# Moving the first pair's weight preparation from the gate product into the output projection

## The chip, the cores and the metric

The kernel runs on one core of one Trainium2 chip. The metric is device time in microseconds (us) of one execution; lower is better. Before the change three timed runs gave a median of 456.75 us (456.43 to 457.58).

The engines are named as in the profile: PE (matrix multiply), PEld (its weight loads), DVE (vector engine), ACT (scalar engine), POOL (GpSimd) and SP (which here only issues DMAs).

## The reference, cut to what matters

One layer of a hybrid decoder: a combined input projection, a block-sparse attention branch and a gated linear recurrence branch, a sigmoid merge, an output projection added to the residual, and at the end a gated per-layer embedding. The change touches only the last two lines:

```python
        merged = jax.nn.sigmoid(gate_a) * ya + jax.nn.sigmoid(gate_b) * yb
        h = h + merged.astype(dt) @ w_out[i]                      # output projection, 512 x 1024 by 1024 x 1024

        ple = (p[i] @ w_ple[i]) * jax.nn.sigmoid(h @ w_ple_gate[i])   # embedding (K = 256) and the gate's product
        h = h + ple
```

## The kernel before, in words

Everything is kept transposed: 1024 features in eight blocks of 128 partitions, 512 tokens along the free axis. Each fp32 matrix product is made from three fp32r matmuls: both operands are split into a high and a low part (ACT copies x to the rounded type for the high part, DVE subtracts it from x for the low part), and hi*hi, lo*hi and hi*lo are added up in PSUM. In names, `h` and `l` at the end stand for the two parts: `w40h`, `w40l` are the parts of the fourth weight set of pair 0.

**Output projection** (the loop `for i, n in enumerate(PAIRED)`): eight blocks in the order h0, h4, h1, h5, h2, h6, h3, h7, each 24 matmuls of 512 columns. After each block DVE adds the residual (`hf`), and `pairs_of_h` makes sums and splits of the two blocks of a pair (tiles `b`, `bl`, `bt`, `bu`) that the gate's product will use.

**The gate's product** (the loop `for p in range(4)`) uses a seven-product scheme: output blocks p and p+4 form a pair, the inner dimension and the tokens are halved, and seven products of 12 matmuls of 256 columns replace eight. The products are numbered 1 to 7. They add up in three PSUM banks, `ba` (1, 2), `bb` (6, 7, 4) and `bc` (5, 3). Between certain products a partial sum must be read out of a bank before the next product adds to it: after product 1 ACT copies `ba` (`keep`), after product 6 DVE makes `keep` from `bb`, after product 7 DVE makes `keep2` (L1214), and an output that is complete is read by DVE (L1159) before the next product of that bank. PE follows the hand-written `order`; for pair 0 it is E0, 1, 5, 6, 2, 7, E1, 4, 3, where E0 and E1 are the small embedding products of six matmuls of 512 columns. `merge` finishes an output: sum, sigmoid on ACT, times the embedding (L1163), plus `hf` (L1164, on POOL, for the last pair on DVE), DMA out.

**The weights of a pair** (`pairs_of_weights`): two raw 512 KB blocks (`wf72` to `wf79` for the four pairs) are loaded by DMAs that POOL's queue issues into four buffers. From them come seven sets: `w1` (products 1 and 2, straight from the first block), the sums `s12` (products 5 and 6; first on POOL, L1046, then on DVE, L1047) and `s34` (products 7 and 3; first on POOL, L1053, then on DVE, L1054), and `w4` (product 4, straight from the second block). Each set is split by ACT (L1037) and DVE (L1038). For pair 0 the sets `w3` and `w4` carry a dependency, order only, that keeps them behind the last step of `pairs_of_h`.

PE's order is fixed by the program text. The order on the other engines comes from a scheduler that ranks by program order, priorities (`AHEAD`) and such order-only dependencies. Each engine runs its queue strictly in order, so an instruction that waits holds up everything behind it.

Of the kernel before, what the change touches and what calls it, by code (L numbers as in the profile page):

```python
# [15 lines left out]
OP = mybir.AluOpType  # L16
# [49 lines left out]
def hybrid_layer_kernel(  # L66
# [961 lines left out]
    def pairs_of_weights(p):  # L1028
        r0, r1 = wraw[late[1] + 2 * p], wraw[late[1] + 2 * p + 1]
        a11, a12, a21, a22 = [r[:, 4 * i:4 * i + 4] for r in (r0, r1) for i in range(2)]  # L1030
        s12 = pb[:, 6:8].rearrange("p a (k c) -> p a k c", k=4)
        s34 = pb[:, 8:10].rearrange("p a (k c) -> p a k c", k=4)

        def both(src, tag, name, shape, late_=False):
            h_ = unit(tag[0], name + "h", R, shape)
            l_ = unit(tag[1], name + "l", R, shape)
            first = A.activation(h_, src, AF.Copy)  # L1037
            second = V.tensor_tensor(l_, src, h_.bitcast(F32), op=OP.subtract)  # L1038
            if late_:
                held(first)  # L1040
                behind(first, edge[-2])
                behind(second, edge[-1])
            return h_, l_

        w1 = both(r0, ("wh", "wl"), f"w1{p}", (128, KD, 128))
        G.tensor_tensor(s12[:, 0], a21, a22, op=OP.add)  # L1046
        second = V.tensor_tensor(s12[:, 1], s12[:, 0], a11, op=OP.subtract)  # L1047
        if p:
            behind(second, edge[-1])
        wt[p] = {1: [t[:, 0:4] for t in w1], 2: [t[:, 4:8] for t in w1]}  # L1050
        yield
        w2 = both(s12, ("wh", "wl"), f"w2{p}", (128, 2, 4, 128))
        G.tensor_tensor(s34[:, 0], a11, a21, op=OP.subtract)  # L1053
        V.tensor_tensor(s34[:, 1], a12, s12[:, 1], op=OP.subtract)  # L1054
        wt[p].update({5: [t[:, 0] for t in w2], 6: [t[:, 1] for t in w2]})
        yield
        w3 = both(s34, ("wh", "wl"), f"w3{p}", (128, 2, 4, 128), p == 0)
        wt[p].update({7: [t[:, 0] for t in w3], 3: [t[:, 1] for t in w3]})
        yield
        w4 = both(a22, ("YB", "YB"), f"w4{p}", (128, 4, 128), p == 0)  # L1060
        wt[p][4] = w4
        yield

    firsts = {}
# [62 lines left out]
    for i, n in enumerate(PAIRED):  # L1127
        ws = weight(w_o[n])
        xres = unit("T", f"xres{n}")
        nc.sync.dma_start(xres, xT[n])  # L1130
        ps = bank("mm", f"h{n}")
        mm3(ps, ws[0], ws[1], mh, ml, KD)
        hf[n] = unit("H", f"hf{n}")
        with tc.high_priority(offset=AHEAD if n == 7 else 0):
            V.tensor_tensor(hf[n], ps, xres, op=OP.add)
        if i == 6:
            small_weights(0)
        if n < 4:
            halves = pairs_of_h(n)
        next(halves)  # L1140
        if i == 3:
            for k in range(2):
                nc.sync.dma_start(pb[:, 8 + k], pT[:, k])
                h_ = unit("A", f"ph{k}", R)
                l_ = unit("A", f"pl{k}", R)
                split(h_, l_, pb[:, 8 + k])
                ph.append(h_)
                pl.append(l_)
        if i == 5:
            preps[0] = pairs_of_weights(0)  # L1150
        if i >= 5:
            w_load(late[1] + i - 3)
        if 5 <= i < 7:
            next(preps[0])

    def merge(n, c, ps, pes, t, plus=None):
        if plus is not None:
            with tc.high_priority(offset=AHEAD):
                V.tensor_tensor(t[:, c], ps, plus, op=OP.add)  # L1159
            ps = t[:, c]  # L1160
        A.activation(t[:, c], ps, AF.Sigmoid)  # L1161
        yield
        V.tensor_tensor(t[:, c], t[:, c], pes[:, c], op=OP.mult)  # L1163
        (V if n % 4 == 3 else G).tensor_tensor(t[:, c], t[:, c], hf[n][:, c], op=OP.add)  # L1164
        nc.sync.dma_start(out[n][:, c], t[:, c])

    for p in range(4):
# [29 lines left out]
        for step in order:  # L1197
# [4 lines left out]
            elif step == "E0r":  # L1202
                ple(pe0, n0, rh)
            elif step == "E0l":
                ple(pe0, n0, lh)
            else:
                product(step)
            with tc.high_priority(offset=AHEAD):
# [4 lines left out]
                elif step == 7:  # L1213
                    V.tensor_tensor(keep2, bb, keep[:, lh], op=OP.add)  # L1214
            if step == 2:
                ends[2] = merge(n0, lh, ba, pe0, t0)
                next(ends[2])
            elif step == 4:
                ends[4] = merge(n1, lh, bb, pe1, t1, keep[:, lh])
                next(ends[4])  # L1220
            elif step == 3:
                ends[3] = merge(n0, rh, bc, pe0, t0, keep[:, rh])
                next(ends[3])
            if 5 in order[:order.index(step) + 1] and 7 in order[:order.index(step) + 1] and "c22" not in ends:
                ends["c22"] = merge(n1, rh, bc, pe1, t1, keep2)
                next(ends["c22"])
            ready = {2: ("E0", "E0l"), 3: ("E0", "E0r"), 4: ("E1",), "c22": ("E1",)}
            for e in list(ends):
                if ends[e] is not None and any(x in order[:order.index(step) + 1] for x in ready[e]):
                    next(ends[e], None)  # L1230
                    ends[e] = None
            if p == 0 and step == 1:
                next(preps[0])
            if p == 0 and step == 6:
                next(preps[0])
                small_weights(n1, True)
            if p == 1 and step in (5, 7):
                small_weights(n0 + 1 if step == 5 else n1 + 1, True)
            if p < 3 and step == 2:
# [73 lines left out]
```

## Time and profile before

| what | before |
|---|---|
| median of 3 runs | 456.75 us (456.43 to 457.58) |
| profiled execution | 456.08 us, span of its instructions 454.2 us, 1.9 us around it |
| PE busy | 446.4 us (98%) |
| DVE / ACT / POOL busy | 335.0 / 289.0 / 59.0 us |
| granted TensorE clock | 1.00 |
| output projection, blocks h2, h6, h3, h7 | 373.5 to 395.3 us |
| pair 0 of the gate's product | 395.3 to 410.6 us |
| last matmul starts | 449.80 us |

Times inside the trace count from the start of the span. In a timeline each row is start, duration, engine, line, operation, output<-inputs, shape; what stands in brackets is the engine's idle time before it and who ended it. Rows of one engine that follow each other closely overlap a little, so the cost of an instruction in a full queue is the distance to the next start and not its duration. Buffer numbers are left out of names: `hf` is any of the eight `hf` tiles.

### The profile page before, as it was taken

How to read it: one execution, taken by the hardware profiler on the slowest of the kernel's cores; microseconds unless marked ns; L12 is line 12 of the kernel's file. 1: busy time of each engine (PE TensorE's matmuls, PEld its weight loads, DVE VectorE, ACT ScalarE, POOL GpSimd, SP SyncE). 2: the span in 40 equal slices, each digit the busy share in tenths (PEclk: the TensorE clock that was granted, in tenths of full speed). 3: DMA queues.
4: the chain of work that ended last, by engine and by line, in shares of the span. 5: the costliest groups of instructions: out<-in, count | busy, mean ns of one | idle time of the engine just before them, and what ended most of it. 6: DMA issues, size and time to landing. Idle time of an engine off the chain costs nothing. (4 is left out here: it accounts for less than half of the span.)

```text
span 454.2 us, 8517 instructions
## 1 busy us (share of the span) xinstructions
PE 446.4 (98%) x3186; PEld 374.4 (82%) x3186; DVE 335.0 (74%) x679; ACT 289.0 (64%) x560; POOL 59.0 (13%) x97
## 2 busy tenths in 40 slices
PE   9999999999999999999999999999999999989996
PEld 8888888788888888878887888878888888879995
DVE  5869593876898795949976875454479769888844
ACT  5958564737679985969877996783234434365421
POOL 1000100000000000010000000101220113133520
PEclk9999999999999999999999999999999999999999
DMA  7802333257492536152435353554731542222111
GB/s 247 330 1 95 139 110 111 93 194 180 184 248 66 179 78 210 35 164 95 142 103 157 123 141 117 163 148 139 267 95 53 180 139 92 94 100 86 48 48 47
DMA packets 32713, 59.53 MB, mean 131 GB/s; under 512 B 7072, under 2 KB 18592, under 8 KB 32672
## 3 DMA queue, kind: packets, MB, share of 16 engines
q0 software_dynamic: 9056, 32.51, 21.3%
q1 hardware_dynamic: 23472, 26.47, 19.8%
q8 instruction: 25, 0.41, 0.4%
q14 instruction: 16, 0.13, 0.1%
q10 hardware_dynamic: 144, 0.01, 0.0%
HBM read 48.74 MB, written 4.98 MB: 118 GB/s over the span
## 5 line engine op out<-in xcount | busy, mean ns | idle before, releaser
L224 ACT ACTIVATE wh<-wf 128x1024 fp32r<-128x1024 f32 (+1 forms) x70 | 67.0, 957 | 63.2 <-issue 9.8
L225 DVE TENSOR_TENSOR wl<-wf,wh 128x1024 fp32r<-128x1024 f32 (+1 forms) x70 | 77.9, 1112 | 34.0 <-ACT wh L224 33.7
L264 POOL DMA_DIRECT2D wf<-in_w_tr_dram x30 | 15.9, 529 | 171.9 <-DVE wl L225 105.8
L290 PE MATMUL ga<-xh,wh 128*128 128x512 f32 x64 | 25.4, 396 | 0.1
L828 ACT ACTIVATE pb<-pb,ps 128x128 f32<-128x128 f32 (+3 forms) x32 | 17.7, 553 | 11.8 <-DVE ps L826 11.6
L290 PE MATMUL gb<-xh,wh 128*128 128x512 f32 x64 | 25.1, 393 | 0.0
L290 PE MATMUL ga<-xh,wl 128*128 128x512 f32 x64 | 24.9, 390 | 0.0
L290 PE MATMUL ga<-xl,wh 128*128 128x512 f32 x64 | 24.9, 389 | 0.0
L290 PE MATMUL gb<-xl,wh 128*128 128x512 f32 x64 | 24.9, 389 | 0.0
L290 PE MATMUL gb<-xh,wl 128*128 128x512 f32 x64 | 24.9, 389 | 0.0
L290 PE MATMUL h<-mh,wh 128*128 128x512 f32 x64 | 24.9, 389 | 0.0
L290 PE MATMUL h<-ml,wh 128*128 128x512 f32 x64 | 24.9, 389 | 0.0
L290 PE MATMUL h<-mh,wl 128*128 128x512 f32 x64 | 24.9, 389 | 0.0
L826 DVE CUSTOM_DVE_ANT_0 pb<-s,bias 128x128 f32<-128x128 f32 (+3 forms) x28 | 13.0, 495 | 10.5 <-PE lpa L559 5.4
L1161 ACT ACTIVATE sg<-sg 128x256 f32<-128x256 f32 x12 | 4.9, 414 | 20.3 <-DVE sg L1159 20.3
L830 ACT ACTIVATE pb<-pb,ps 128x128 f32<-128x128 f32 (+3 forms) x32 | 16.3, 550 | 0.2 <-DVE ps L829 0.2
L538 ACT ACTIVATE hx<-hx 128x512 f32<-128x512 f32 x24 | 14.8, 623 | 1.4 <-DVE hx L537 1.3
L264 POOL DMA_DIRECT2D wf<-in_w_up_dram x16 | 8.6, 539 | 53.7 <-DVE wl L225 50.8
L833 DVE STREAM_TRANSPOSE pb<-pb 128x512 f32<-128x512 f32 x20 | 13.8, 696 | 2.0 <-ACT pb L830 2.0
L264 POOL DMA_DIRECT2D wf<-in_w_tok_dram x8 | 4.4, 550 | 79.5 <-DVE wl L225 67.6
L290 PEld LDWEIGHTS ga<-xh,wh 128*128 128x128 f32 x64 | 12.0, 188 | 3.3 <-DVE bg3s L487 0.5
L290 PEld LDWEIGHTS gb<-xh,wh 128*128 128x128 f32 x64 | 12.0, 188 | 2.8 <-DVE hk L513 0.4
(941 smaller groups left out, 1427.6 us busy)
## 6 DMA issues: line engine op xcount, KB each, us to landing
wf<-in_w_tr_dram POOLq DMA_DIRECT2D x30, 512.0 KB, 4.5
wf<-in_w_tok_dram POOLq DMA_DIRECT2D x8, 512.0 KB, 3.5
wf<-in_w_up_dram POOLq DMA_DIRECT2D x16, 256.0 KB, 3.0
wf<-in_w_o_dram POOLq DMA_DIRECT2D x8, 512.0 KB, 4.3
wf<-in_w_g_dram POOLq DMA_DIRECT2D x8, 512.0 KB, 3.6
wf<-in_w_tok_dram SPq DMA_DIRECT2D x6, 512.0 KB, 6.9
pb<-pb SPq DMA_DIRECT2D x64, 48.0 KB, 2.9
bias<-in_ed_dram SPq DMA_DIRECT2D x8, 256.0 KB, 4.6
```

The source lines that it names most:

```text
L224: A.activation(hi, src, AF.Copy)
L225: V.tensor_tensor(lo, src, hi.bitcast(F32), op=OP.subtract)
L264: (G if len(wraw) >= FAR else nc.sync).dma_start(raw, ap)
L290: dense.append(PE.matmul(ps, a[:, k, :], b[k], start=(n == 0), stop=(n == tot - 1)))
L538: A.activation(x, x, AF.Exp)
L826: in_order(V.tensor_tensor_reduce(p_, s_[:, so:so + nk], T[j][:, nk - 1::-1], -1.0, 3e38, OP.add, OP.min, st[:, 0:1]))
L828: A.activation(p_, p_, AF.Exp, bias=st[:, 0:1], scale=-1.0, accum_out=st[:, 1:2])
L830: A.activation(p_, p_, AF.Copy, scale=st[:, 2:3])
L833: V.transpose(z[:, :, b_, :].rearrange("p b (n c) -> p b n c", c=32), pb[:, b_].rearrange("p (n b c) -> p b n c", b=4, c=32))
L1161: A.activation(t[:, c], ps, AF.Sigmoid)
```

## The change

In `pairs_of_weights`, pair 0 now takes its own way after the sets 1, 5 and 6: it makes set 4 at once (in buffers of tag `Q`), then set 7 alone (tag `SG`), then set 3 alone, called `w5` here (tags `wh`, `wl`), and only set 3 carries the order-only dependency. The generator's steps are called ahead of the matmuls of blocks i = 5, 6 and 7 (h6, h3, h7) instead of behind the blocks 5 and 6 and inside pair 0. The embedding weights of n = 4 (`pwh4`, `pwl4`) are made at i = 7 instead of after product 6. One more thing is changed: in the last pair the left half of the embedding product (E0l) writes to a bank of its own (`pe3l`, tag `mm`) instead of the bank that holds the right half. No matmul is added or taken away.

```diff
@@ pairs_of_weights
-        w3 = both(s34, ("wh", "wl"), f"w3{p}", (128, 2, 4, 128), p == 0)
+        if p == 0:
+            wt[p][4] = both(a22, ("Q", "Q"), f"w4{p}", (128, 4, 128))
+            yield
+            wt[p][7] = both(s34[:, 0], ("SG", "SG"), f"w3{p}", (128, 4, 128))
+            yield
+            wt[p][3] = both(s34[:, 1], ("wh", "wl"), f"w5{p}", (128, 4, 128), True)
+            yield
+            return
+        w3 = both(s34, ("wh", "wl"), f"w3{p}", (128, 2, 4, 128))
         wt[p].update({7: [t[:, 0] for t in w3], 3: [t[:, 1] for t in w3]})
         yield
-        w4 = both(a22, ("YB", "YB"), f"w4{p}", (128, 4, 128), p == 0)
-        wt[p][4] = w4
+        wt[p][4] = both(a22, ("YB", "YB"), f"w4{p}", (128, 4, 128))
         yield
@@ for i, n in enumerate(PAIRED)
         nc.sync.dma_start(xres, xT[n])
+        if i == 5:
+            preps[0] = pairs_of_weights(0)
+            next(preps[0])
+        elif i == 6:
+            next(preps[0])
+            next(preps[0])
+            small_weights(0)
+        elif i == 7:
+            next(preps[0])
+            small_weights(4)
         ps = bank("mm", f"h{n}")
         mm3(ps, ws[0], ws[1], mh, ml, KD)
...
-        if i == 6:
-            small_weights(0)
...
-        if i == 5:
-            preps[0] = pairs_of_weights(0)
         if i >= 5:
             w_load(late[1] + i - 3)
-        if 5 <= i < 7:
-            next(preps[0])
@@ merge: pes is now a function that gives the bank
-        V.tensor_tensor(t[:, c], t[:, c], pes[:, c], op=OP.mult)
+        V.tensor_tensor(t[:, c], t[:, c], pes()[:, c], op=OP.mult)
@@ for p in range(4)
             elif step == "E0l":
-                ple(pe0, n0, lh)
+                pe2 = bank("mm", f"pe{n0}l")
+                ple(pe2, n0, lh)
...
-            if p == 0 and step == 1:
-                next(preps[0])
             if p == 0 and step == 6:
                 next(preps[0])
-                small_weights(n1, True)
```

**Place one: DVE between block h3's residual add and that of h7.** `hf3` and `hf7` are the residual adds; `w4x` are the weights of product 4 of pair x; `pb` rows of L1085 (L1092 after) are token differences of `hf3`. Before:

```order
L1135 TENSOR_TENSOR hf3_4261<-h3_4236,xres3_4234 128x512
L1085 TENSOR_TENSOR pb_70<-hf3_4261 128x256
L1038 TENSOR_TENSOR w20l_4278<-pb_70,w20h_4277 128x1024
L225 TENSOR_TENSOR b2l_4172<-hf3_4261,b2h_4171 128x256
L225 TENSOR_TENSOR bt3l_4271<-pb_70,bt3h_4270 128x256
L1135 TENSOR_TENSOR hf7_4312<-h7_4287,xres7_4285 128x512
```

Now:

```order
L1152 TENSOR_TENSOR hf3_4276<-h3_4251,xres3_4234 128x512
L1092 TENSOR_TENSOR pb_70<-hf3_4276 128x256
L1125 TENSOR_TENSOR pwl4_4297<-pb_70,pwh4_4296 128x512
L1038 TENSOR_TENSOR w20l_4237<-pb_70,w20h_4236 128x1024
L1038 TENSOR_TENSOR w41l_4483<-wf75_4232,w41h_4482 128x512
L225 TENSOR_TENSOR b2l_4172<-hf3_4276,b2h_4171 128x256
L225 TENSOR_TENSOR bt3l_4281<-pb_70,bt3h_4280 128x256
L1038 TENSOR_TENSOR w42l_4641<-wf77_4486,w42h_4640 128x512
L1152 TENSOR_TENSOR hf7_4325<-h7_4300,xres7_4289 128x512
```

Three subtractions of 512 columns stand here that stood behind product 6 before: the embedding's `pwl4`, and the product-4 weights of pairs 1 and 2. The last needs the raw block `wf77`. Two more (`w40l` and, of half its width, `w30l`) stand one block earlier, ahead of the residual add of h2.

**Place two: DVE from the copy after product 6 of pair 0 to the first completed output.** `keep0` is that copy; L1214 (L1226 now) makes `keep2`; L1159 (L1170 now) reads a completed output out of PSUM. Before:

```order
L1212 TENSOR_TENSOR keep0_4330<-g01_4324,keep0_4330 128x256
L1038 TENSOR_TENSOR w40l_4380<-wf73_4136,w40h_4379 128x512
L1118 TENSOR_TENSOR pwl4_4385<-pb_70,pwh4_4384 128x512
L1047 TENSOR_TENSOR pb_70<-pb_70,wf74_4182 128x512
L1038 TENSOR_TENSOR w11l_4405<-wf74_4182,w11h_4404 128x1024
L1038 TENSOR_TENSOR w41l_4479<-wf75_4232,w41h_4478 128x512
L1163 TENSOR_TENSOR sg0_4328<-sg0_4328,pe0_4326 128x256
L1054 TENSOR_TENSOR pb_70<-wf74_4182,pb_70 128x512
L1214 TENSOR_TENSOR pb_70<-g01_4324,keep0_4330 128x256
L1038 TENSOR_TENSOR w21l_4435<-pb_70,w21h_4434 128x1024
L1038 TENSOR_TENSOR w42l_4637<-wf77_4482,w42h_4636 128x512
L1159 TENSOR_TENSOR sg4_4329<-g02_4325,pb_70 128x256
```

Now:

```order
L1224 TENSOR_TENSOR keep0_4343<-g01_4337,keep0_4343 128x256
L1038 TENSOR_TENSOR w50l_4389<-pb_70,w50h_4388 128x512
L1047 TENSOR_TENSOR pb_70<-pb_70,wf74_4182 128x512
L1038 TENSOR_TENSOR w11l_4409<-wf74_4182,w11h_4408 128x1024
L1054 TENSOR_TENSOR pb_70<-wf74_4182,pb_70 128x512
L1174 TENSOR_TENSOR sg0_4341<-sg0_4341,pe0_4339 128x256
L1226 TENSOR_TENSOR pb_70<-g01_4337,keep0_4343 128x256
L1038 TENSOR_TENSOR w21l_4439<-pb_70,w21h_4438 128x1024
L1170 TENSOR_TENSOR sg4_4342<-g02_4338,pb_70 128x256
```

Between `keep0` and `keep2` seven instructions stood and now five do; between `keep2` and the first completed output two stood and now one does.

**Place three: POOL's queue at the raw blocks of pairs 1 to 3.** L1046 and L1053 are POOL's sums for the weight sets, L264 the loads. Before:

```order
L264 DMA wf75_4232<-in_w_g_dram 128x1024
L264 DMA wf76_4283<-in_w_g_dram 128x1024
L1046 TENSOR_TENSOR pb_70<-wf75_4232 128x512
L1053 TENSOR_TENSOR pb_70<-wf74_4182,wf75_4232 128x512
L264 DMA wf77_4482<-in_w_g_dram 128x1024
L264 DMA wf78_4640<-in_w_g_dram 128x1024
L1164 TENSOR_TENSOR sg0_4328<-sg0_4328,hf0_3981 128x256
L264 DMA wf79_4642<-in_w_g_dram 128x1024
```

Now:

```order
L264 DMA wf75_4232<-in_w_g_dram 128x1024
L1053 TENSOR_TENSOR pb_70<-wf74_4182,wf75_4232 128x512
L264 DMA wf76_4287<-in_w_g_dram 128x1024
L264 DMA wf77_4486<-in_w_g_dram 128x1024
L1046 TENSOR_TENSOR pb_70<-wf75_4232 128x512
L264 DMA wf78_4644<-in_w_g_dram 128x1024
L264 DMA wf79_4646<-in_w_g_dram 128x1024
L1175 TENSOR_TENSOR sg0_4341<-sg0_4341,hf0_3981 128x256
```

L1053 of pair 1 moves up, ahead of the loads of `wf76` and `wf77`, and the load of `wf79` now stands ahead of the first `sg0` sum. The buffers rotate in another order too: `wf77` goes where `wf72` lay (last read by `w10l`), `wf78` where `wf75` lay (last read by `w41l` and POOL's L1046 of pair 1), `wf79` where `wf74` lay (last read by DVE's L1054 of pair 1). On ACT the split `w43h`, which waits for `wf79`, changes places with `w31h` and stands ahead of it; behind both come one sigmoid and the copy `keep1`.

More of the change, by code (lines that the diff above doesn't have):

```diff
@@ L1215, in hybrid_layer_kernel @@
             if step == 2:
-                ends[2] = merge(n0, lh, ba, pe0, t0)
+                pe2 = pe0
+                ends[2] = merge(n0, lh, ba, lambda: pe2, t0)
                 next(ends[2])
             elif step == 4:
-                ends[4] = merge(n1, lh, bb, pe1, t1, keep[:, lh])
+                ends[4] = merge(n1, lh, bb, lambda: pe1, t1, keep[:, lh])
                 next(ends[4])
             elif step == 3:
-                ends[3] = merge(n0, rh, bc, pe0, t0, keep[:, rh])
+                ends[3] = merge(n0, rh, bc, lambda: pe0, t0, keep[:, rh])
                 next(ends[3])
             if 5 in order[:order.index(step) + 1] and 7 in order[:order.index(step) + 1] and "c22" not in ends:
-                ends["c22"] = merge(n1, rh, bc, pe1, t1, keep2)
+                ends["c22"] = merge(n1, rh, bc, lambda: pe1, t1, keep2)
                 next(ends["c22"])
```

## The prediction

> **What bounds the kernel now.** I read the page first (span, busy shares, clock), then PE's own waits in the last 125 us, then PE's timeline at each of them, then the queues of the engines named there.
>
> ```profile
> span 454.2 us, 8517 instructions
> PE 446.4 (98%) x3186; PEld 374.4 (82%) x3186; DVE 335.0 (74%) x679; ACT 289.0 (64%) x560; POOL 59.0 (13%) x97
> PEclk9999999999999999999999999999999999999999
> ```
>
> PE is the bound, at full granted clock, and the change keeps all its matmuls. So it can only win the gaps between matmuls, and only from the region it touches. PE's waits after 330 us:
>
> ```profile
> PE g L1184 <- DVE pb L1214: 1.1, 1, 1.1
> PE g L1184 <- DVE sg L1159: 0.9, 1, 0.9
> PE g L1184 <- ACT keep L1210: 0.2, 1, 0.2
> ```
>
> Three waits, all in the gate's product. These rows count from the modelled end of the last matmul; the time really lost shows in the distance of the starts, in PE's timeline:
>
> ```profile
> 396.63 0.28 PE L1184 MATMUL g<-b0h,w10h 128*128 128x256 f32 x1
> ...
> 404.75 0.39 PE L290 MATMUL pe<-pl,pwh 128*128 128x512 f32 x1
> 404.98 0.39 PE L290 MATMUL pe<-ph,pwl 128*128 128x512 f32 x1
> 406.50 0.39 PE L1184 MATMUL g<-bu0h,w40h 128*128 128x256 f32 x1 [1.12 <-DVE pb L1214]
> ...
> 407.92 0.28 PE L1184 MATMUL g<-bt3h,w40l 128*128 128x256 f32 x1
> 409.11 0.39 PE L1184 MATMUL g<-bl0h,w30h 128*128 128x256 f32 x1 [0.92 <-DVE sg L1159]
> 409.33 0.28 PE L1184 MATMUL g<-bl0l,w30h 128*128 128x256 f32 x1
> ...
> 413.41 0.28 PE L1184 MATMUL g<-bt3h,w21l 128*128 128x256 f32 x1
> 413.87 0.39 PE L1184 MATMUL g<-bl0h,w11h 128*128 128x256 f32 x1 [0.18 <-ACT keep L1210]
> ...
> 448.79 0.28 PE L1184 MATMUL g<-bl3h,w13l 128*128 128x256 f32 x1
> 449.11 0.38 PE L290 MATMUL pe<-ph,pwh 128*128 128x256 f32 x1
> ```
>
> A 512-column matmul follows the last after 0.23 (404.75 to 404.98), a 256-column one after 0.12 (34 steps from 409.33 to 413.41), and the first after a stall holds PE 0.10 longer (409.11 to 409.33). The losses:
> - Before product 4 of pair 0: 406.50 - 404.98 - 0.23 + 0.10 = 1.39.
> - Before product 3 of pair 0: 409.11 - 407.92 - 0.12 + 0.10 = 1.17.
> - Before product 2 of pair 1: 413.87 - 413.41 - 0.12 + 0.10 = 0.44.
> - Before E0l of pair 3: 449.11 - 448.79 - 0.12 + 0.10 = 0.30.
>
> Together 3.30 us. That is the ceiling of the gain; what follows is how much of it stays.
>
> **Products 4 and 3 of pair 0: DVE's queue.** Both waits end with a DVE instruction that stood behind weight splits:
>
> ```profile
> 401.21 0.42 DVE L1212 TENSOR_TENSOR keep<-g,keep 128x256 f32<-128x256 f32 x1 [1.05 <-PE g L1184]
> ...
> 402.75 0.68 DVE L1047 TENSOR_TENSOR pb<-pb,wf 128x512 f32<-128x512 f32 x1
> 403.36 1.22 DVE L1038 TENSOR_TENSOR w11l<-wf,w11h 128x1024 fp32r<-128x1024 f32 x1
> 404.49 0.68 DVE L1038 TENSOR_TENSOR w41l<-wf,w41h 128x512 fp32r<-128x512 f32 x1
> ...
> 406.03 0.41 DVE L1214 TENSOR_TENSOR pb<-g,keep 128x256 f32<-128x256 f32 x1
> 406.36 1.76 DVE L1038 TENSOR_TENSOR w21l<-pb,w21h 128x1024 fp32r<-128x1024 f32 x1
> ...
> 408.64 0.41 DVE L1159 TENSOR_TENSOR sg<-g,pb 128x256 f32<-128x256 f32 x1
> ```
>
> In a full queue a 512-column subtraction costs 0.61 (402.75 to 403.36), a 1024-column one 1.13 (403.36 to 404.49), a 256-column one 0.34 (406.03 to 406.36, rounded up). `keep` at 401.21 was started by PE, so the clock starts there. With the new queue (place two) `keep2` starts at 401.21 + 0.34 + 3 x 0.61 + 1.13 + 0.34 = 404.85 instead of 406.03, and ends at 405.26. PE took it 0.06 after its end before (406.44 to 406.50), so 405.32; PE is ready at 404.98 + 0.23 = 405.21. Left over: 0.11 and perhaps the slow first matmul, **0.15** of 1.39.
>
> Then `w21l`, then the first completed output: 404.85 + 0.34 + 1.13 = 406.32, its end and hand-over 406.79. PE comes to product 3 at 405.32 + 0.10 + 12 x 0.12 = 406.86, so nothing is left if `w21l` takes 1.22. It took 1.76 before, because POOL was at work: at that length 407.33, and 0.5 is left. Which? Rows where DVE and POOL meet:
>
> ```profile
> 374.45 1.57 POOL L1046 TENSOR_TENSOR pb<-wf 128x512 f32<-128x512 f32 x1 [3.07 <-DMA wf<-in_w_g_dram]
> 374.78 1.52 DVE L1097 TENSOR_TENSOR pb<-hf,hf 128x256 f32<-128x256 f32 x1
> 376.22 2.31 DVE L225 TENSOR_TENSOR wl<-wf,wh 128x1024 fp32r<-128x1024 f32 x1
> 378.82 0.57 POOL L264 DMA_DIRECT2D wf<-in_w_g_dram  x1 [1.38 <-DVE wl L225]
> ...
> 427.40 0.88 DVE L1047 TENSOR_TENSOR pb<-pb,wf 128x512 f32<-128x512 f32 x1
> 427.69 1.19 POOL L1164 TENSOR_TENSOR sg<-sg,hf 128x256 f32<-128x256 f32 x1
> ...
> 433.19 0.74 POOL L1164 TENSOR_TENSOR sg<-sg,hf 128x256 f32<-128x256 f32 x1 [4.31 <-DVE sg L1163]
> ```
>
> With POOL first, a DVE instruction of 0.42 took 1.52 (1.1 lost). With DVE first, POOL's sum took 1.19 instead of 0.74. DVE reads PSUM at 401.21 in its usual 0.42. After the change POOL's `sg0` sum stands behind the load of `wf79`, which waits for L1054's end (403.90 + 0.68 = 404.6). A load starts 0.29 after the end of what it waits for (378.53 to 378.82) and holds POOL for 0.57, so the sum is due near 405.4 and `w21l` at 405.2: DVE first. I take the short one and leave **0.1** of 1.17.
>
> The Trainium skill, "SBUF — State Buffer", section "Who interferes with whom", says that a VectorE instruction with two SBUF inputs and a GpSimd instruction that reads SBUF exclude each other, whoever issues first holding the pair to its end. The rows above agree in both orders. By that rule the remainder at product 3 would be nothing; by a mere repeat of the 1.76 row it would be 0.5 and the gain 0.4 smaller. The rule also speaks against the change, since POOL's L1053 of pair 1 now meets a full DVE queue.
>
> **Blocks h6, h3, h7: what the earlier place costs.** The work moved must fit into DVE's idle time:
>
> ```profile
> 390.03 0.69 DVE L1135 TENSOR_TENSOR hf<-h,xres 128x512 f32<-128x512 f32 x1 [0.48 <-PE h L290]
> ...
> 395.47 0.69 DVE L1135 TENSOR_TENSOR hf<-h,xres 128x512 f32<-128x512 f32 x1 [1.39 <-PE h L290]
> ...
> 397.81 0.42 DVE L225 TENSOR_TENSOR bt3l<-pb,bt3h 128x256 fp32r<-128x256 f32 x1
> ```
>
> Added ahead of `hf7`: five subtractions of 512 columns, 5 x 0.61 = 3.05, and one meeting with POOL (L1053), 1.1. Idle there: 0.48 + 1.39 = 1.87. So `hf7` slips from 395.47 by 2.3 and the token split `bt3l` ends at 398.23 + 2.3 = 400.5. PE wants it in the eleventh matmul of product 6, at 396.63 + 34 x 0.12 = 400.71. It just fits; each 0.1 more than 0.15 goes to PE. If the meeting with POOL falls into a gap or a PSUM read, 1.1 is to spare; if a second one is added, 0.9 is lost. I take **0.1**. ACT's added splits lie in its long waits and are costed at nothing: ACT was 64% busy. The moved splits themselves are hidden under the 24 matmuls of each block; if that cover were gone they would cost the 3.05.
>
> **Product 2 of pair 1: ACT behind a load.** `keep1` frees the bank:
>
> ```profile
> 410.79 1.06 ACT L1037 ACTIVATE w31h<-pb 128x1024 fp32r<-128x1024 f32 x1 [0.95 <-POOL sg L1164]
> 412.61 0.63 ACT L1037 ACTIVATE w43h<-wf 128x512 fp32r<-128x512 f32 x1 [0.76 <-DMA wf<-in_w_g_dram]
> 413.15 0.40 ACT L1161 ACTIVATE sg<-sg 128x256 f32<-128x256 f32 x1
> 413.45 0.36 ACT L1210 ACTIVATE keep<-g 128x256 f32<-128x256 f32 x1
> ```
>
> The times from issue to landing of the last nine raw loads, shortest, median and longest:
>
> ```profile
> DMA to landing us min/median/max: 3.4/3.5/5.6
> ```
>
> `keep1` was late because `w43h` waited for `wf79`, the load with the 5.6. It was issued at 412.6 - 5.6 = 407.0, just behind that of `wf78`, which `w41l` at 404.49 had released. Now `w41l` stands ahead of `hf7`, so `wf78` leaves around 397, and `wf79`, issued at 404.6 + 0.3 = 404.9, should take the median 3.5 and land at 408.4. Behind it stand `w43h` (0.54 to the next start), now `w31h` (1.0), the sigmoid (0.30) and `keep1` (0.36): with the hand-over 410.7. PE wants it at 406.86 + 36 x 0.12 = 411.2. So 0.5 of slack, and with 5.6 us for the load a loss of 1.6. I expect **0.15** left of the 0.44.
>
> **E0l of pair 3** waited for DVE to read the other half of its bank; with its own bank nothing holds it: **0** left of 0.30, and all of it if the gap had another cause, since no row names one. DVE's last two instructions follow PE's end as before.
>
> **The sum.** 3.30 - 0.15 - 0.1 - 0.1 - 0.15 = 2.8 us, so the profiled execution goes from 456.08 to 453.3. That execution is 0.67 below the median of the runs shown, 456.75; on that scale **454.0 us**. From the bounds: all gaps closed 453.4; POOL first at `w21l` 454.4.
>
> **The rivals.**
> - *The load holds `keep1`* (chance 0.14). `w31h` is now behind the load's wait, for it that it took 5.6 before, against it that it is alone in the queue now. At 5.6: 2.8 + 0.15 - 1.6 = 1.3 gained, 455.4.
> - *DVE's backlog reaches PE at product 6* (0.13). For it the slack of 0.2 on a chain of twenty instructions; against it that the meeting with POOL may be cheaper. A second 1.1 gives 454.9.
> - *The stalls stay* (0.06). The subtractions removed were not what ended last, or others take their place: PE's wait row names `keep2` only as the last one seen. Then 456.7.
> - *Slower* (0.05). `w42l` stands ahead of `hf7` on DVE and waits, through `w42h`, for `wf77`, which is issued only behind `w10l`. `w10l` ends four instructions (0.34 + 3 x 0.61 = 2.2) ahead of `hf3`, and `hf3` comes at 390.03 + 2 x 0.61 + 1.1 - 0.48 = 391.9; so it is issued near 390.0 and at 3.5 lands at 393.5, `w42h` ends at 394.1, and `w42l`'s turn comes at 397.8 - 0.61 = 397.2. That is 3.1 to spare. The longest landing of all POOL's raw loads stands in this row:
>
> ```profile
> DMA to landing us min/median/max: 2.7/3.7/7.5
> ```
>
> At 7.5 about 0.8 is lost; from about 9.5 the whole gain is eaten, and at 12 the time is 459. The place is real, the price needs a load slower than any seen.
>
> **The numbers.** A difference under 0.3% (1.4 us) can't be told from none. The forecast has 0.62 and lies well over that bound; with the backlog case (454.9, 0.4%) faster is 0.75. The load case and the lasting stalls make 0.20 for no change, the slow load 0.05 for slower. The range goes from all gaps closed less run-to-run spread, 453.1, to most of the load case, 456.0.
>
> **What would show it.** In the changed trace: product 4 of pair 0 starts about 1.2 and product 3 about 2.3 earlier, each following its predecessor by at most 0.35; `hf7` starts near 397.7 and no gap stands inside product 6; `keep1` ends before 411.2 and `w43h` before 409.5; `w21l` takes 1.2 and POOL's `sg0` sum longer than 0.74; E0l follows its predecessor by 0.12; DVE is nearly without idle time from 379 to 397. I am wrong if PE's waits name L1226 or L1170 with over 0.5, if `hf7` comes later than 398, if ACT's `w43h` waits for its load past 410, or if a gap appears in blocks h3 or h7, where I cost nothing.

## The result and the profile after

| | before | after | ratio (95%) |
|---|---|---|---|
| first comparison, 5 runs each | 456.43 us (455.89 to 457.58) | 454.12 us (452.84 to 454.60) | 0.9939 (0.9915 to 0.9964) |
| second comparison, 11 and 6 runs | 457.38 us (455.65 to 458.48) | 453.58 us (452.40 to 454.12) | 0.9915 (0.9892 to 0.9938) |
| profiled execution | 456.08 us, span 454.2 | 454.12 us, span 452.3 | |

The change makes the kernel faster by 0.6 to 0.85%. The forecast was 454.0 us. The page of the kernel after begins:

```profile
span 452.3 us, 8522 instructions
PE 446.4 (99%) x3186; PEld 375.2 (83%) x3186; DVE 335.6 (74%) x680; ACT 289.2 (64%) x561; POOL 59.7 (13%) x97
PEclk9999999999999999999999999999999999999999
```

PE is busy for the same 446.4 us at the same clock, and the list of PE's waits after 330 us, which had three rows before, is empty. The places of those waits in PE's timeline (start, duration, engine, line, operation, output<-inputs, shape):

```profile
406.10 0.39 PE L290 MATMUL pe<-ph,pwl 128*128 128x512 f32 x1
406.41 0.38 PE L1195 MATMUL g<-bu0h,w40h 128*128 128x256 f32 x1
406.63 0.28 PE L1195 MATMUL g<-bu0l,w40h 128*128 128x256 f32 x1
...
407.83 0.28 PE L1195 MATMUL g<-bt3h,w40l 128*128 128x256 f32 x1
407.97 0.36 PE L1195 MATMUL g<-bl0h,w50h 128*128 128x256 f32 x1
408.16 0.28 PE L1195 MATMUL g<-bl0l,w50h 128*128 128x256 f32 x1
...
412.24 0.28 PE L1195 MATMUL g<-bt3h,w21l 128*128 128x256 f32 x1
412.36 0.28 PE L1195 MATMUL g<-bl0h,w11h 128*128 128x256 f32 x1
...
447.18 0.28 PE L1195 MATMUL g<-bl3h,w13l 128*128 128x256 f32 x1
447.30 0.28 PE L290 MATMUL pe3l<-ph,pwh 128*128 128x256 f32 x1
```

Product 4 follows E1 after 0.31 instead of 1.52, product 3 follows after 0.14 instead of 1.19, and product 2 of pair 1 and E0l follow after the normal 0.12. What is left is 0.18 before product 4 (0.08 of gap and 0.10 of slow first matmul) and 0.09 before product 3: 0.27 of the 3.30.

**Where to measure.** The two spans differ by 1.9 us only, but the last matmul starts 3.0 us earlier if one counts from the first matmul of the output projection. Up to there both kernels run the same program, and yet the two profiled executions reach it 1.12 us apart. The first matmul of block h0 and the last matmul of the program, in PE's timeline of the kernel before:

```profile
351.75 0.39 PE L290 MATMUL h<-mh,wh 128*128 128x512 f32 x1
...
449.80 0.28 PE L290 MATMUL pe<-ph,pwl 128*128 128x256 f32 x1
```

and of the kernel after:

```profile
352.87 0.39 PE L290 MATMUL h<-mh,wh 128*128 128x512 f32 x1
...
447.90 0.28 PE L290 MATMUL pe3l<-ph,pwl 128*128 128x256 f32 x1
```

That is 98.05 us before and 95.03 us after, 3.02 less; the terms above give 3.30 - 0.27 = 3.03. I call this distance the **last stretch** from here on. It is what tells experiments of a few tenths apart: it was 95.03 in both profiles of the kernel after (e10), and the largest change seen in a part that an edit did not touch was 0.13 (e1), while single times scatter by 2 us and more.

### The profile page after: what moved, and what is told of

Same layout as the page of the kernel before. It is cut to its first block, busy times and chain, and to the rows that moved or that the text cites. A ratio compares the mean times of both kernels' runs of the same rounds, so it can differ in the third digit from the quotient of the medians.

```text
span 452.3 us, 8522 instructions
## 1 busy us (share of the span) xinstructions
PE 446.4 (99%) x3186; PEld 375.2 (83%) x3186; DVE 335.6 (74%) x680; ACT 289.2 (64%) x561; POOL 59.7 (13%) x97
## 4 chain that ended last, share of the span: by engine, by line
PE 62%; issue 21%; DVE 5%; DMA 5%; ACT 3%; SPq 2%; POOL 1%; POOLq 0%; DVEq 0%; ACTq 0%
PE h L290 10%; PE g L1195 9%; PE ga L290 9%; PE ub L290 5%; PE ua L290 5%; PE av L420 5%; PE bi L420 5%; PE aq L420 4%; DMA wf<-in_w_tr_dram 4%; PE gb L290 2%; PE pe L290 2%; SPq L844 2%; ACT wh L224 1%; PE bq L290 1%; PE bf L290 1%
## 5 line engine op out<-in xcount | busy, mean ns | idle before, releaser
L264 POOL DMA_DIRECT2D wf<-in_w_tr_dram x30 | 15.8, 528 | 172.5 <-DVE wl L225 108.2
L264 POOL DMA_DIRECT2D wf<-in_w_up_dram x16 | 8.6, 538 | 53.8 <-DVE wl L225 50.8
L264 POOL DMA_DIRECT2D wf<-in_w_tok_dram x8 | 4.4, 550 | 80.0 <-DVE wl L225 68.0
```

Of the source, the lines that this page charges most:

```text
L264: (G if len(wraw) >= FAR else nc.sync).dma_start(raw, ap)
```

## The experiments

All kernels compute the whole output. The last stretch of each, from one profiled execution each (h0 and last matmul: their starts in us), and its single time or median:

```
kernel                          h0      last    stretch   against   time
before                        351.75   449.80    98.05    (before)  456.08
after                         352.87   447.90    95.03    -3.02     454.12
e1  before, own bank for E0l  352.45   450.32    97.87    -0.18     456.61
                                                         (after)
e2  w42l twice                352.46   447.49    95.03     0.00     453.74
e3  w20l and w42l twice       352.59   447.55    94.96    -0.07     453.91
e4  load of wf77 twice        351.38   447.61    96.23    +1.20     453.96
e5  POOL's sum first          352.51   447.97    95.46    +0.43     454.25
e6  pwl4 back                 353.16   449.22    96.06    +1.03     455.46
e7  w40 in YB                 353.88   448.91    95.03     0.00     455.27
e8  sets 7 and 3 whole        353.32   450.79    97.47    +2.44     457.04
e9  five more subtractions    351.56   449.02    97.46    +2.43     455.41
e10 after, unchanged          352.10   447.13    95.03     0.00     453.58 (6 runs)
e11 keep2 first               352.17   447.20    95.03     0.00     453.67 (6 runs)
e12 hf7 three times           351.56   446.95    95.39    +0.36     453.19
```

The kernel before, run beside them, took 456.38 us (one run, e1 to e4), 457.37 (one run, e5 to e8 and e12) and 457.38 (median of 11, e9 to e11).

### e1: the bank of E0l alone

```diff
             elif step == "E0l":
-                ple(pe0, n0, lh)
+                pe2 = bank("mm", f"pe{n0}l")
+                ple(pe2, n0, lh)
```

> Kernel before, plus only the own bank for the left half of the last pair's embedding product (E0l). Theory (the gap before E0l is PE waiting for DVE to read the other half of the same bank): the first matmul of E0l starts 0.12 us after its predecessor instead of 0.32, the next one follows at 0.12 as well, so 0.30 us less and nothing else; the gaps before products 4 and 3 of pair 0 and product 2 of pair 1 stay at 1.4, 1.2 and 0.4 within 0.15. Rival (the gap is the price of changing to the embedding's operands): the distance stays at 0.32. A difference of 0.3 us cannot be read from the times, only from the trace.

The last rows of this kernel's product ahead of E0l, in PE's timeline:

```profile
449.60 0.28 PE L1184 MATMUL g<-bl3h,w13l 128*128 128x256 f32 x1
449.72 0.28 PE L290 MATMUL pe3l<-ph,pwh 128*128 128x256 f32 x1
```

0.12 instead of 0.32: the gap was the shared bank, and it is gone with it. Products 4 and 3 of pair 0 lose 1.39 and 1.18, as before to 0.01. Product 2 of pair 1 lost 0.57 here instead of 0.44, so the stretch is shorter by 0.18 and not by 0.30: ACT's `w43h` waits there for the load of `wf79`, which took 5.7 us instead of 5.6.

### e2 and e3: more work ahead of hf7

```diff
-            second = V.tensor_tensor(l_, src, h_.bitcast(F32), op=OP.subtract)
+            second = [V.tensor_tensor(l_, src, h_.bitcast(F32), op=OP.subtract)
+                      for _ in range(2 if name == "w42" else 1)][-1]          # e3: in ("w20", "w42")
```

> Kernel after, with the subtraction for w42l made twice: one more 512-column subtraction (0.60 us) on DVE directly ahead of hf7, nothing else moved up to there. Theory (the last token split bt3l had about 0.4 us of slack before the matmul of product 6 that reads it): hf7 starts 0.60 later against block h7's matmuls, PE stops before the matmul that reads bt3l for 0.2 us and restarts slowly, 0.3 lost in all, and products 4 and 3 lose no more than in the kernel after. Rival (DVE's queue behind block h3 is not what PE waits for in product 6): no gap in product 6.

> Kernel after, with the subtractions for w20l (1024 columns, 1.13 us) and w42l (512 columns, 0.60 us) made twice, the second time directly ahead of hf7: 1.73 us more in DVE's queue there. Theory: slack 0.4, so PE loses 1.73 - 0.40 + 0.10 = 1.4 us in product 6, where the previous kernel loses 0.3; everything behind moves with PE. Rival (DVE's queue ahead of hf7 has more room, or PE is held elsewhere): no gap in product 6, or one under 0.5.

Neither lost anything: both of my numbers were wrong. PE read `bt3l` at 401.42 in e2 and at 401.55 in e3, with no gap. The rows of DVE and POOL show why. First the kernel after, at the two places where POOL's sums meet DVE, and on to `bt3l`:

```profile
387.74 1.29 POOL L1053 TENSOR_TENSOR pb<-wf,wf 128x512 f32<-128x512 f32 x1 [6.08 <-DMA wf<-in_w_g_dram]
387.84 1.47 DVE L1099 TENSOR_TENSOR pb<-hf,pb 128x256 f32<-128x256 f32 x1
...
395.81 1.66 POOL L1046 TENSOR_TENSOR pb<-wf 128x512 f32<-128x512 f32 x1 [4.20 <-DVE w20l L1038]
396.24 1.51 DVE L225 TENSOR_TENSOR b2l<-hf,b2h 128x256 fp32r<-128x256 f32 x1
...
398.61 0.68 DVE L1152 TENSOR_TENSOR hf<-h,xres 128x512 f32<-128x512 f32 x1
...
400.94 0.42 DVE L225 TENSOR_TENSOR bt3l<-pb,bt3h 128x256 fp32r<-128x256 f32 x1
```

and the same places in e3:

```profile
386.66 1.38 POOL L1053 TENSOR_TENSOR pb<-wf,wf 128x512 f32<-128x512 f32 x1 [5.32 <-DVE pwl L1125]
387.52 0.80 DVE L1099 TENSOR_TENSOR pb<-hf,pb 128x256 f32<-128x256 f32 x1
...
395.25 0.42 DVE L225 TENSOR_TENSOR b2l<-hf,b2h 128x256 fp32r<-128x256 f32 x1
```

In the kernel after L1053 began 0.10 ahead of L1099 and held it for its whole length: 1.47 instead of the 0.42 that it takes alone, 1.05 lost. In e3 it had begun 0.86 ahead, and DVE lost 0.38. In e3 the second `w20l` also kept POOL's L1046 from starting (it waits for the last reader of its buffer), so `b2l` took its 0.42 and 1.1 came back; 0.38 of that went again behind `hf7`, where L1046 met L1099 (0.80 instead of 0.42). Together 0.67 + 1.09 - 0.38 = 1.38 of the added 1.73 came back, so `bt3l` ended only 0.31 later against product 1 than in the kernel after (3.92 us behind its start instead of 3.61). I had added work to a queue and taken the meetings with POOL as fixed. They aren't: eleven of the profiles have this L1053 early, and the DVE row that met it was 0.38 to 0.5 longer than alone in nine of them and 1.05 to 1.1 longer in two (after and e7). In eight of the nine POOL's row begins ahead of h6's residual add `hf`, in the ninth (e6) 0.07 behind its start; that add, which has one input in PSUM, kept its 0.67 or 0.68 beside POOL, so that a good part of L1053 was over when the next DVE row came. In the profile of after L1053 began 0.61 behind the start of that add.

### e4: the load that `w42l` waits for comes later

```diff
-            (G if len(wraw) >= FAR else nc.sync).dma_start(raw, ap)
+            for _ in range(2 if len(wraw) == 77 else 1):
+                (G if len(wraw) >= FAR else nc.sync).dma_start(raw, ap)
```

> Kernel after, with the 512 KB load of wf77 issued twice into the same buffer, the second waiting for the first: the block is there about 4 us later, and no instruction changes place on any engine. Theory (the slower rival of the prediction: w42l stands ahead of hf7 on DVE and waits for this load; measured slack of w42l 1.7 us, then 0.4 in product 6): the block lands near 399.6 on the clock of the profiled kernel after instead of 395.6, w42l starts near 400.1 instead of 398.0, hf7 2.1 later, PE loses 2.1 - 0.4 + 0.1 = 1.8 us in product 6, so most of the gain of the change is gone. Rival (the wait is covered): under 0.3 lost.

Here the slower rival of the prediction is brought about. ACT's `w42h` and DVE's `w42l` wait, and PE after them:

```profile
397.35 0.63 ACT L1038 ACTIVATE w42h<-wf 128x512 fp32r<-128x512 f32 x1 [5.08 <-DMA wf<-in_w_g_dram]
...
398.02 0.69 DVE L1039 TENSOR_TENSOR w42l<-wf,w42h 128x512 fp32r<-128x512 f32 x1 [1.79 <-ACT w42h L1038]
...
400.96 0.42 DVE L225 TENSOR_TENSOR bt3l<-pb,bt3h 128x256 fp32r<-128x256 f32 x1
...
400.54 0.28 PE L1196 MATMUL g<-bt3h,w20h 128*128 128x256 f32 x1
401.43 0.39 PE L1196 MATMUL g<-bt3l,w20h 128*128 128x256 f32 x1 [0.61 <-DVE bt3l L225]
```

PE lost 0.88 here and 0.34 at the start of product 6, 1.2 in all, where I had 1.8. The path is the one that the rival named. The size was off because the first of the two loads left 0.66 earlier against PE than in the kernel after (388.93 with product 1 at 396.26, against 391.08 with product 1 at 397.75; L1053 had held DVE for 0.4 instead of 1.05), so `hf7` came 1.5 later and not 2.1. Product 6 began 0.06 after the end of `hf7`; no row names what it waited for, and that it was the bank which `hf7` reads is only argued.

### e12: the slack of product 6 measured

```diff
         with tc.high_priority(offset=AHEAD if n == 7 else 0):
-            V.tensor_tensor(hf[n], ps, xres, op=OP.add)
+            for _ in range(3 if n == 7 else 1):
+                V.tensor_tensor(hf[n], ps, xres, op=OP.add)
```

> Kernel after, with block h7's residual add made three times on DVE (two more instructions of 512 columns, 0.6 to 0.7 us each, into the same tile); the order on DVE is otherwise that of the kernel after. Theory (PE reads the last token split bt3l 4.07 us after the start of product 1, a hand-over takes 0.05; bt3l ended at 2.95 in the second profile of the kernel after and at 3.61 in the first, by how long POOL's L1053 held DVE): it now ends 1.3 later, at 4.25 to 4.9, and PE loses in product 6 what its end lies behind 4.02, plus 0.10 for the slow first matmul: 0.3 to 1.0 us, and to within 0.1 the number that this run's own end of bt3l gives. Products 4 and 3 as in the kernel after. Rival (room for some us more ahead of product 6): nothing lost.

DVE and PE in this kernel, in which product 1 began at 396.44:

```profile
396.60 2.13 DVE L1153 TENSOR_TENSOR hf<-h,xres 128x512 f32<-128x512 f32 x3
...
400.39 0.41 DVE L225 TENSOR_TENSOR bt3l<-pb,bt3h 128x256 fp32r<-128x256 f32 x1
...
400.39 0.28 PE L1196 MATMUL g<-bt3h,w20h 128*128 128x256 f32 x1
400.86 0.39 PE L1196 MATMUL g<-bt3l,w20h 128*128 128x256 f32 x1 [0.19 <-DVE bt3l L225]
401.08 0.28 PE L1196 MATMUL g<-bt3h,w20l 128*128 128x256 f32 x1
```

`bt3l` ended 4.36 after the start of product 1 (400.80), 0.34 past 4.02. PE lost 0.35 before its matmul and 0.10 behind it: 0.45 where the rule gives 0.44. (The stretch is longer by 0.36 only, because the gap of 0.08 before product 4 went.) The same rule gives 5.12 - 4.02 + 0.10 = 1.20 for e4, which lost 1.2, and nothing for e2 (3.70) and e3 (3.92). So the mechanism of the second rival, DVE's backlog reaching PE, holds; what was missing for it was 0.4 us in the profile of after (3.61) and 1.1 in its repetition (2.95).

### e9: the attempt that told less

```diff
-            second = V.tensor_tensor(l_, src, h_.bitcast(F32), op=OP.subtract)
+            second = [V.tensor_tensor(l_, src, h_.bitcast(F32), op=OP.subtract)
+                      for _ in range(3 if name == "w20" else 2 if name in ("w41", "w42") else 1)][-1]
```

> Kernel after, with five subtractions made again on DVE: w20l (1.13), w41l (0.60) and w42l (0.60) directly ahead of hf7, and w20l once more (1.13) directly behind hf7, 3.46 us in all ahead of the last token split bt3l, twice the 1.73 us of the kernel with w20l and w42l twice, which lost nothing. There bt3l ended 0.16 before the matmul that reads it, and a hand-over takes 0.05. Theory (that kernel used up the slack, because POOL's sums met DVE for 1.8 us less than in the kernel after): the further 1.73 us go to PE but for that 0.1, plus 0.1 for the slow first matmul, so 1.7 us lost in product 6 (1.0 to 2.4, since the meetings with POOL vary by 0.7). Rival (DVE's queue ahead of product 6 has room for some us more): under 0.5.

PE did lose 1.74, the expected number, but for another reason than expected. The longest of its waits:

```profile
PE g L1195 <- DVE w20l L1038: 1.5, 1, 1.5
```

The third `w20l` stood behind `hf7`, where PE already wants to read that tile in product 5. The stop came at product 5, from the tile that I had written again, and `bt3l` was no longer what ended last. Products 4 and 3 lost another 0.7 beyond the kernel after, which makes up the 2.43. This run says nothing about the slack; e12 replaced it.

### e5: POOL's sum ahead of the load

```diff
+            if len(wraw) in after_:
+                behind(dma, after_[len(wraw)])          # the load of wf79
...
-        (V if n % 4 == 3 else G).tensor_tensor(t[:, c], t[:, c], hf[n][:, c], op=OP.add)
+        total = (V if n % 4 == 3 else G).tensor_tensor(t[:, c], t[:, c], hf[n][:, c], op=OP.add)
+        if n == 0 and c == lh:
+            after_[79] = total
```

> Kernel after, with POOL's first sg0 sum ordered ahead of the load of wf79 again, as in the kernel before. Theory (what makes w21l long is that POOL's sum begins first): the sum starts about 0.1 after L1174's end, ahead of w21l, takes 0.75 instead of 1.29, and w21l takes 1.76 instead of 1.21; the completed output behind it comes 0.55 later and PE loses 0.45 more before product 3 of pair 0 than in the kernel after. w43h moves behind w31h and the sigmoid on ACT; its load leaves 0.6 later than in the kernel after and lands in time, so nothing is lost before product 2 of pair 1. Rival (the length of w21l has another cause): w21l stays at 1.2 and product 3 loses nothing more.

POOL's sum and DVE's `w21l`, first of e5:

```profile
405.76 0.73 POOL L1179 TENSOR_TENSOR sg<-sg,hf 128x256 f32<-128x256 f32 x1 [8.53 <-DVE sg L1178]
...
405.92 1.65 DVE L1042 TENSOR_TENSOR w21l<-pb,w21h 128x1024 fp32r<-128x1024 f32 x1
```

then of the kernel after:

```profile
405.94 0.41 DVE L1226 TENSOR_TENSOR pb<-g,keep 128x256 f32<-128x256 f32 x1
406.28 1.21 DVE L1038 TENSOR_TENSOR w21l<-pb,w21h 128x1024 fp32r<-128x1024 f32 x1
406.80 1.29 POOL L1175 TENSOR_TENSOR sg<-sg,hf 128x256 f32<-128x256 f32 x1
407.41 0.41 DVE L1170 TENSOR_TENSOR sg<-g,pb 128x256 f32<-128x256 f32 x1
```

With POOL 0.16 ahead, POOL took 0.73 and DVE 1.65; with DVE 0.52 ahead, DVE took 1.21 and POOL 1.29. Nothing else on DVE moved up to there. The expected 0.45 came as 0.43. The load that the exchange held back took 4.3 us instead of 3.4 and still landed in time.

### e6: the embedding weights of n = 4 back behind product 6

```diff
         elif i == 7:
             next(preps[0])
-            small_weights(4)
...
             if p == 0 and step == 6:
                 next(preps[0])
+                small_weights(n1, True)
```

> Kernel after, with the embedding weights of n = 4 (pwh4, pwl4) made after product 6 of pair 0 again: pwl4 stands between keep0 and keep2 on DVE, and POOL's first sg0 sum again ahead of the load of wf79. Theory: keep2 comes 0.60 later, so PE loses 0.5 to 0.6 more before product 4 than the 0.18 of the kernel after; w21l is again behind POOL's sum and takes 1.76, 0.45 more before product 3; hf7 comes 0.6 earlier, which gains nothing; 1.0 to 1.1 lost in all. Rival (keep2 is not held by the number of subtractions ahead of it): product 4 as in the kernel after.

1.03 lost, as expected in sum, but in other parts. Product 4 lost 0.61 more than in the kernel after (0.79 in all), which is the one subtraction of 0.60 put back ahead of `keep2`. Product 3 lost 0.15 more instead of 0.45: POOL's sum began 0.77 ahead of `w21l`, most of its length was over, and `w21l` took 1.42. Product 2 of pair 1 lost 0.30, which I had not expected: `wf79` left at 407.47 behind the sum, `w43h` waited for it 0.61, and behind it `keep1` came late again, as in the kernel before. So the mechanism of the first rival, the load that holds `keep1`, is real. The place of the load goes with its length: behind POOL's first `sg0` sum it took 4.2 to 5.7 us from issue to landing in six profiles (before 5.6, e1 5.7, e5 4.3, e6 4.8, e8 5.2, e9 4.2), ahead of it 3.4 to 3.7 in eight. Why was not tried, and the place alone does not set the price: e5 and e9 lost nothing before product 2 of pair 1.

### e7: set 4 of pair 0 in other buffers

```diff
-            wt[p][4] = both(a22, ("Q", "Q"), f"w4{p}", (128, 4, 128))
+            wt[p][4] = both(a22, ("YB", "YB"), f"w4{p}", (128, 4, 128))
```

> Kernel after, with one pair of buffers changed back: w40h and w40l in tag YB instead of Q. They can then be written only when block h7 has begun, w41 and w42 move one place back, w42l now stands ahead of keep0 on DVE and w42h ahead of ACT's copy of the bank ba (keep), and on POOL the load of wf77 leaves behind L1046, near 397.6 on the clock of the profiled kernel after instead of 391. Theory: a landing time of 3.5 to 4.4 puts that copy at 402.0 to 402.9, against PE's wish for it at 402.06, so product 2 of pair 0 starts 0 to 0.9 late, I say 0.5, and at 5.6 it would be 2.1; keep0 and keep2 move with it. Rival (the tag only saves buffers and the order does not matter): no gap before product 2, products 4 and 3 as in the kernel after.

No loss, where I had expected 0.5: the stretch is 95.03 again. `w40l` left block h6, so DVE reached `w20l`, and POOL behind it, earlier against PE than I had it. The load left 0.92 ahead of product 1's start (398.75), and ACT's split did not wait for it:

```profile
401.57 0.63 ACT L1037 ACTIVATE w42h<-wf 128x512 fp32r<-128x512 f32 x1
402.10 0.37 ACT L1222 ACTIVATE keep<-g 128x256 f32<-128x256 f32 x1
```

The copy ended 3.72 behind product 1's start, and PE wanted it at 4.31. Here it did not matter that `w41l` instead of `w42l` stood last ahead of `hf7`: `w42l` now stood behind it, but still ahead of `keep0`, out of the way of `keep2`.

### e8: sets 7 and 3 in one piece

```diff
-            wt[p][7] = both(s34[:, 0], ("SG", "SG"), f"w3{p}", (128, 4, 128))
             yield
-            wt[p][3] = both(s34[:, 1], ("wh", "wl"), f"w5{p}", (128, 4, 128), True)
+            w3 = both(s34, ("wh", "wl"), f"w3{p}", (128, 2, 4, 128), True)
+            wt[p].update({7: [t[:, 0] for t in w3], 3: [t[:, 1] for t in w3]})
             yield
```

> Kernel after, with the weight sets 7 and 3 of pair 0 kept as one set of 1024 columns behind the token splits, as in the kernel before (set 4 and pwl4 stay early). Between keep0 and keep2 stands then w30l with 1.13 instead of w50l with 0.60, and POOL's L1053 of pair 1, no longer released early, falls into this stretch. Theory: keep2 at least 0.53 later, up to 1.1 more where L1053 meets DVE, so PE loses 0.5 to 1.6 more before product 4 than the kernel after, and 0.45 more before product 3 because POOL's sum is again ahead of w21l; hf7 comes up to 1.6 earlier. Rival (set 4 and pwl4 alone made the gain): products 4 and 3 as in the kernel after.

Most of the gain is gone: 2.44 of 3.02. PE's waits, and the rows of POOL and DVE between `keep0` and `keep2`:

```profile
PE g L1195 <- DVE pb L1226: 1.3, 1, 1.3
PE g L1195 <- ACT keep L1222: 0.4, 1, 0.4
```

```profile
404.42 1.68 POOL L1053 TENSOR_TENSOR pb<-wf,wf 128x512 f32<-128x512 f32 x1 [8.14 <-DVE w30l L1038]
404.86 2.32 DVE L1038 TENSOR_TENSOR w11l<-wf,w11h 128x1024 fp32r<-128x1024 f32 x1
```

`w30l` with its 1024 columns costs 0.53 there, and it frees the buffer of POOL's L1053 just then: `w11l` takes 2.32 instead of 1.22. Product 4 loses 1.35 more than in the kernel after. Product 7 loses 0.31 because it waits for `w30l` too (it goes on at 404.39, 0.05 after the end of `w30l`), and product 2 of pair 1 loses 0.68, behind a load of 5.2 us; I had expected neither. Product 3 loses 0.15 more, not 0.45. Splitting the set therefore does two things: it halves what stands ahead of `keep2`, and it moves the meeting of L1053 with DVE to block h3, where it made DVE late (in the kernel after its rows follow each other without a pause there) but cost PE nothing.

### e10: the kernel after once more

> The kernel after, unchanged. Theory (up to the first matmul of the output projection the two kernels run the same program, and executions differ there by up to 2.5 us; behind it they repeat): from the first matmul of block h0 to the start of the last matmul 95.03 us within 0.15, whatever the whole span is (98.05 in the kernel before); the median of the timed runs 2 to 3.5 us below that of the kernel before. Rival (the change itself moves the early part, by 1.1 us as in the two profiles): h0 starts again 1.1 later than the 351.75 of the profile of before, within 0.2.

The last stretch is 95.03 again, and h0 starts at 352.10, 0.35 behind the profile of before and not 1.12. The median fell by 3.8 us, a little more than the 2 to 3.5 that I had expected. The rival that the change itself delays the early part is out.

### e11: `keep2` ahead of the multiplication

```diff
+            behind(second, summed[-1])          # L1174 of n = 0, left half, behind keep2
...
-                    V.tensor_tensor(keep2, bb, keep[:, lh], op=OP.add)
+                    summed.append(V.tensor_tensor(keep2, bb, keep[:, lh], op=OP.add))
```

> Kernel after, with one pair of DVE instructions exchanged in pair 0: keep2 (L1226) ahead of the multiplication by the embedding (L1174), not behind it. Theory (what is left of the stall before product 4 is keep2 coming 0.1 late): keep2 starts 0.33 earlier, the 0.18 left before product 4 goes, PE then comes 0.18 earlier to product 3, where the completed output is no earlier than in the kernel after, so that 0.1 to 0.2 is lost there: 0 to 0.2 gained, nothing that the times can show. Rival (the rest before product 4 is the switch of banks or operands, not keep2): product 4 follows its predecessor by 0.31 as in the kernel after.

PE at products 4 and 3 in this kernel:

```profile
405.41 0.39 PE L290 MATMUL pe<-ph,pwl 128*128 128x512 f32 x1
405.63 0.28 PE L1199 MATMUL g<-bu0h,w40h 128*128 128x256 f32 x1
...
406.94 0.28 PE L1199 MATMUL g<-bt3h,w40l 128*128 128x256 f32 x1
407.28 0.36 PE L1199 MATMUL g<-bl0h,w50h 128*128 128x256 f32 x1
```

Product 4 follows without a gap, and product 3 gives all of it back: the stretch is 95.03. What is left of the stall is the length of DVE's queue up to the first completed output, and an exchange inside that queue only moves it. The ratio to the kernel before is 0.9916 (0.9894 to 0.9938), that of the kernel after beside it 0.9915.

## Why the prediction was right

| term | left over, predicted | left over, measured |
|---|---|---|
| product 4 of pair 0 (1.39) | 0.15 | 0.18 |
| product 3 of pair 0 (1.17) | 0.10 | 0.09 |
| backlog at product 6 | 0.10 | 0 |
| product 2 of pair 1 (0.44) | 0.15 | 0 |
| E0l of pair 3 (0.30) | 0 | 0 |
| sum gained | 2.8 | 3.02 |

To compare the rows below with the prediction's, 1.12 us are taken off the times of the kernel after, by which its h0 started later.

- **The ceiling.** Counting the starts of matmuls and not the listed waits gave 3.30. The listed waits make 2.2, and the E0l gap isn't among them; e1 shows that it was there and what it was.
- **`keep2`.** Predicted at 404.85; L1226 started at 405.94 - 1.12 = 404.82. The sum of queue distances was good to 0.03, and e6 confirms its unit: one subtraction put back, 0.61 lost.
- **`w21l`.** I took the 1.22 against the 1.76 because DVE should be first. It was, by 0.52, and took 1.21. POOL's sum took 1.29 instead of 0.74, as said. e5 turned the order around and got 1.65. The rule of the Trainium skill, "SBUF — State Buffer", section "Who interferes with whom", is borne out by these two pairs of rows in both orders; it also says that a VectorE instruction with at most one SBUF input, outside of the modes that use two ports, is not concerned, and L1170 at 407.41, with one of its two inputs in PSUM, took its 0.41 while POOL's sum ran. The starts in the rows do not always tell who comes first, though. In e4 `b2l` began 0.22 ahead of POOL's sum (394.08 against 394.30) and yet took 1.81 instead of 0.42, while the sum took 1.30, about its length alone (1.29). In e9 a sum of POOL began at 399.86 and took 2.95, while four DVE rows that began between 399.96 and 401.23 kept their usual lengths.
- **`hf7`.** Predicted slip 2.3, to 397.7; it started at 398.61 - 1.12 = 397.49. `bt3l` ended at 401.36 - 1.12 = 400.24 against the predicted 400.5 and PE's need at 400.71. The step that was less sure than it looked is the 1.1 for the meeting with L1053: 1.05 in this profile, 0.38 in most others.
- **`wf79` and `keep1`.** The load was said to leave at 404.9 and land at 408.4. Its row in POOL's timeline, and the rows of `w43h` and `keep1` in ACT's:

```profile
406.25 0.53 POOL L264 DMA_DIRECT2D wf<-in_w_g_dram  x1 [7.92 <-DVE sg L1174]
...
409.64 0.63 ACT L1037 ACTIVATE w43h<-wf 128x512 fp32r<-128x512 f32 x1 [0.62 <-DMA wf<-in_w_g_dram]
...
411.43 0.36 ACT L1222 ACTIVATE keep<-g 128x256 f32<-128x256 f32 x1
```

  It left at 406.25 - 1.12 = 405.13 (the row names L1174, the instruction behind the L1054 that I had counted on), was there within 3.4 and `w43h` began at 408.52; `keep1` ended at 411.79, and PE wanted it at 412.36. The slack was 0.57 where 0.5 was predicted, and none of the 0.15 that I kept back was lost. With the load behind POOL's sum this slack was gone in e6, but not in e5.
- **The slower rival.** I gave `w42l` 3.1 us to spare; it had 1.7, since `w42h` ended at 396.29 and `w42l`'s turn came at 398.01. The load took 4.5 (issued at 391.08) instead of the 3.5 I had used. e4 shows the price beyond that point: what `bt3l` is late, plus 0.10.
- **The time.** On the profiled scale I had 453.3, and the gain was 3.02; the profiled execution after took 454.12 because its early part was 1.12 longer: 456.08 - 3.02 + 1.12 = 454.18. The medians fell by 2.3 us in the first comparison and 3.8 in the second, on either side of 3.0. That the forecast of 454.0 hit the first median to 0.12 is partly luck; the sum by terms, 2.8 against 3.02, is the better measure.

What I did not see is how the parts hang together. I costed five stalls one by one. By e8, undoing the split of the sets 7 and 3 alone takes 2.44 of the 3.02 away again, much of it through the place where POOL's sum meets DVE, and by e7 the buffers of set 4 carry nothing by themselves.

## What to carry to other kernels

A gap of a fully used engine is best sized from the starts of its instructions, and the wait behind it from the distances between starts in the queue of the engine it waits for: both were right here to a few hundredths. Two engines that share something make a queue's length depend on who gets its turn first, so a slack worked out from one profile needs the spread of those meetings on it, and an added instruction can shift a meeting and cost nothing. To tell a change of under 1% apart, measure from a marker just ahead of the changed part.

## What the runs showed of the hardware that I had not expected

Executions of the same program differ in the first 350 us by up to 2.5 us, about as much as the change is worth. The starts of h0 in the table reach from 351.38 (e4) to 353.88 (e7), at full granted clock throughout. The offsets against the profile of before arise in three places and stand still between them (us, at the given times of the profile of before):

```
at us    before  after   e1    e2    e3    e4    e5    e6    e7    e8    e9    e10   e11
 25.2     0.00   0.43   1.49  0.81  0.13  0.20  0.67  0.22  0.53  0.48  0.71  0.86  0.54
128.6     0.00   0.39   1.47  0.81  0.13  0.18  0.67  0.24  0.55  0.45  0.68  0.84  0.53
169.1     0.00   0.53   1.59  1.34  0.31  0.18  0.80  0.77  1.81  0.71  0.85  0.84  0.63
191.4     0.00   0.54   1.60  1.34  0.31  0.19  0.81  0.78  1.82  0.72  0.86  0.85  0.64
255.0     0.00   1.12   0.70  0.71  0.84 -0.35  0.73  1.41  2.10  1.54 -0.18  0.35  0.42
341.8     0.00   1.11   0.70  0.71  0.84 -0.38  0.75  1.40  2.12  1.57 -0.19  0.35  0.42
```

In some of them PE's waits between 125 and 250 us name a cause at the end of the chain, as in e7:

```profile
PE bf L290 <- DVE bg1s L487: 1.0, 1, 1.0
PE o L857 <- DMA pb<-pb: 1.0, 1, 1.0
```

The second waits for the DMAs of the attention. That the loads at the start and those DMAs vary from execution to execution fits the rows; what makes them vary was not tried. From 255 us on, thirteen executions kept their offsets to 0.03, and four different kernels (after twice, e2, e7, e11) ran the last stretch in 95.03.
